# The input projection of an S5 mixer, token-major or feature-major: one stage of a kernel of two transformer blocks

## The chip, the cores and the metric

The kernel runs on one core of a Trainium2 chip. The metric is the device time of one launch in microseconds; less is better. The core has a matrix engine (TensorE, in the profile PE, its weight loads PEld), VectorE (DVE), ScalarE (ACT), GpSimd (POOL) and a queue that issues the transfers (SyncE, SP). Every engine works through its own instructions in order and waits on semaphores for the others.

## What is computed

Two blocks of a float32 model of 1024 tokens and 1024 features: a layer with a gated recurrence and attention, a state-space layer, a feed-forward layer, a mixer layer, and a second feed-forward layer. Only the mixer layer is concerned. Its input projection gives queries, keys, values (512 features each) and u, the input of the S5 mixer. Cut to u:

```python
proj = h @ w_mix_in                       # [1024 tokens, 2048]
q, k, v, u = split(proj, [512, 1024, 1536])
attn = dilated_attention(q, k, v)
# s5_mixer(u): 32 groups of 16 channels, 64 complex states a group
a_bar = exp(dt * a)
b_bar = ((a_bar - 1) / a)[..., None] * b
bu = einsum('bsgc,gpc->bsgp', u, b_bar)
states[t] = a_bar * states[t - 1] + bu[t]  # an associative scan
y = real(einsum('bsgp,gcp->bsgc', states, c)) + d_skip * u
y = gelu(y)
ssm = y * sigmoid(y @ w_glu + b_glu)
mixed = concatenate([attn, ssm]) @ w_mix_out
```

## The kernel before

Activations lie feature-major: eight tiles of 128 features (on partitions) by 1024 tokens, each as a pair (high, low) whose sum is the float32 value, in TensorE's one-pass type. A product is three passes: high times high, high times low, low times high. `proj_fm` makes one tile of 128 output features with the weights as the stationary operand and 512 tokens as the moving one, for all eight feature tiles k.

The mixer layer, `mix_layer`, goes like this. `lead` makes the first two query tiles while the last tokens of the layer before are still being normalised. Then comes the projection to u, then four S5 blocks (`s5_block`) of eight groups, then the other six query and key tiles (`proj_fm`, `stash` spills each as a pair to DRAM), then the values, token-major, then the gating of the S5 output and the attention.

The S5 mixer works on chunks of 8 tokens. The operators of a block of 8 groups (`w1`, `g`, `tp`, `cos`, `sin`, 128 x 1024 each) lie prepared in DRAM and are loaded by SyncE. A block needs its input as `ut`: step and channel on the partitions, group and chunk along the columns. The kernel before gets there in two steps. The projection is token-major: the stationary operand is every eighth token of the activations, so that chunks come out on the partitions, and the weights are the moving operand, 256 columns at a time; then the block transposes U, [chunk, (group, step, channel)], by eight products with the identity.

```python
xh, xl = (get(m, k).rearrange("p (c s) -> p s c", s=8)[:, s, :] for m in "hl")
nc.tensor.matmul(o, xh, wh, start=k == 0, stop=False)
nc.tensor.matmul(o, xh, wl, start=False, stop=False)
nc.tensor.matmul(o, xl, wh, start=False, stop=k == NK - 1)
```

In a block two products, `e` (with `w1`) and `y` (with `tp` and `g`), stand around elementwise work on VectorE: a turn by `cos` and `sin`, a scan along the chunks, a turn back. The block's eight 128 x 1024 tiles are four double tiles of one pool with four buffers, so that a block's loads wait until the block before has released them: the tile of `t1`, `t2` is free when the scan's results are turned back, the other three when the last product `y` is done.

Nobody writes the order of the engines' instructions out: a scheduler sets it from the order of the code, the pools' buffers and its own estimate of times. Weights go through two staging buffers (`wst`), four buffers of high parts and four of low parts; `wload` loads them, scales their rows by a gain on ScalarE (one instruction per feature tile) and splits them. PSUM has two tiles of 1024 columns (`a`) and four of 512 (`b`).

Of the kernel before, what the change touches and what calls it, by code (L numbers as in the profile page):

```python
# [26 lines left out]
# ---------------------------------------------------------------- parameter columns  # L27
# [71 lines left out]
def anchor(K, engine=None):  # L99
    """The last instruction traced on an engine, the tensor engine unless another is given."""  # L100
    for i in reversed(K.nc.cur_bb.bb.instructions):
        if i.engine == (engine or K.pe):
            return i
    return None
# [3 lines left out]
def deferred(K, after):  # L108
    """Loads and fills in the block, which wait for no data, are issued behind `after`
    instead of taking their buffers as soon as one is free."""  # L110
# [13 lines left out]
def marks(K):  # L124
    """The last instructions traced on the engines that do the elementwise work."""
    return [anchor(K, e) for e in (K.act, K.dve, K.pool)]
# [3 lines left out]
def behind(K, ins):  # L130
    """What the block traces is issued behind `ins`, each on its own engine."""
# [6 lines left out]
def split(K, hi, lo, src, eng=None):  # L138
    """hi + lo == src exactly, both in the tensor engine's one-pass type."""
# [4 lines left out]
def scale_rows(K, st, gain, k0, n):  # L144
    """st [128, n, cols] *= the gains of its rows, those of tiles k0 .. k0 + n."""
# [4 lines left out]
def wload(K, src, a, b, gain=None, k0=0):  # L150
    """Weights [128, a, b] with a * b <= 1024 from DRAM, by rows times a gain, as the pair (hi, lo)."""
# [16 lines left out]
def proj_list(K, ps, terms):  # L168
    """ps[f, t] = sum over terms (wh, wl, xh, xl) of w[k, f] x[k, t], three passes each."""
# [12 lines left out]
def lead(K, ws, xt):  # L182
    """Two products of proj_fm at the start of a layer, the first 512 tokens of both ahead of
    the others, which may not be there yet."""
# [11 lines left out]
def transpose_tokens(K, xn, i, XT):  # L196
    """Token tile xn [128 tokens, 1024] -> columns i of the feature-major pair XT."""
# [21 lines left out]
def exp_poly(K, out, x, r, k, ki):  # L219
    """out = exp(x) with x held within +-87, to float32's accuracy; r, k are float and ki  # L220
    integer scratch of x's shape, and out may be x."""
# [14 lines left out]
def softplus(K, out, x, e, s, q, ki):  # L236
    """out = max(x, 0) + log1p(exp(-|x|)); the others are scratch of x's shape (ki integer)."""
# [15 lines left out]
def rsqrt_col(K, out, v, n, scale, eps, mul=1.0, tag="rs"):  # L253
    """out = mul / sqrt(v * scale + eps) on n columns: a first guess from the exponent and
    three Newton steps."""
# [18 lines left out]
def sin_tables(K, pos, cos, sin, ang, n):  # L274
    """cos and sign * sin of the rotary angles, rows as the feature tiles have them."""
# [8 lines left out]
def _parts(*bits):  # L284
    """2 pi as a sum of float32 values, all but the last of so many bits."""
# [11 lines left out]
def reduce_2pi(K, out, ang, n, few=False):  # L297
    """out = ang less a multiple of 2 pi, within +-pi, by steps; n is scratch. `few` says that
    less than 128 turns are taken off."""
# [14 lines left out]
def sin_cos(K, sin, cos, ang, n, sgn, few=False):  # L314
    """sin(sgn * ang) and cos(ang), by steps; n is scratch, and ang may be sin or cos."""
# [7 lines left out]
def conv4(K, out, src, wname, j, nm, bname, copy=False):  # L323
    """Causal conv of 4 taps along tokens for feature tile j of nm (src may be PSUM); with
    `copy` the later taps read a copy of src, which frees it sooner."""
# [11 lines left out]
def attention(K, qb_passes, table, scale, vt, out, p0, ring, chunks):  # L337
    """One head. qb_passes(qb) gives [(stationary [k, 128 queries], moving [k, T keys])];
    table [128, T] is the additive table whose column 896 - 128 qb + key is used;
    vt(kb) is the stationary [128 keys, 64 high | 64 low parts]; out [64, T], whose first  # L340
    partition is p0, takes the transposed result."""
# [51 lines left out]
def layer_a(K, I, XT, get):  # L393
    nc = K.nc
    # feature-major input
# [47 lines left out]
    # low-rank inputs  # L443
# [53 lines left out]
    # gates  # L497
# [14 lines left out]
    # attention operands  # L512
# [81 lines left out]
class Ring:  # L594
    """Runs of columns in turn, from tiles of four rows."""
# [13 lines left out]
class Chunks:  # L609
    """Pairs of transposed probabilities [128, 512] in turn."""  # L610
# [978 lines left out]
def mix_layer(K, I, get, ydram):  # L1589
# [27 lines left out]
    for b in range(4):  # L1617
        s5_block(K, b, U[b])
# [279 lines left out]
```

## Time and profile before

| | us |
|---|---|
| median of 3 runs | 3497.23 |
| fastest and slowest run | 3487.03, 3500.45 |
| span of the profiled execution (first to last instruction) | 3487.5 |
| TensorE busy in the span | 3191.8 (92%) |
| VectorE, ScalarE, GpSimd busy | 2281.8, 1624.8, 741.3 |
| S5 input projection in it | 2267.1 to 2359.6 |
| rest of the stage, to the end of the values | 2359.6 to 2502.1 |

The page gives the span of the profiled execution and no other time of it. Busy time of TensorE includes the overlap of pipelined products, so how fast products follow each other is read from the difference of their starts.

### The profile page before, as it was taken

Reading aid. Unit: us, or ns where it says so; the run is one execution under the profiler, and the core shown is the slowest. Engines: PE = TensorE matmul, PEld = TensorE weight load, DVE = VectorE, ACT = ScalarE, POOL = GpSimd, SP = SyncE. Lnnn points to the kernel's source line nnn. Section 1 sums busy time; section 2 is a strip of 40 time slices with the busy share of each in tenths; the row PEclk is TensorE's granted clock in tenths of the full one; section 3 lists DMA queues with packets and bytes.
Section 4 is the critical chain, followed back from the end, with each engine's and each line's share of the span. In section 5 each row is a group of like instructions: output and inputs, shape, how many; then the busy total and the mean of one; then the engine's idle time right before and its main releaser. Section 6 shows DMA issues by size and latency. Waiting matters only on the chain. (4 is left out here: it accounts for less than half of the span.)

```text
span 3487.5 us, 42834 instructions
## 1 busy us (share of the span) xinstructions
PE 3191.8 (92%) x15848; PEld 2670.7 (77%) x15848; DVE 2281.8 (65%) x3859; ACT 1624.8 (47%) x2971; POOL 741.3 (21%) x455
## 2 busy tenths in 40 slices
PE   8999898999998889879999999799999799999997
PEld 7878776878786867667778777698877578888776
DVE  6537785274747555888775789705676965555998
ACT  5436534253545432455555443523376565554442
POOL 0000010121222111432233434100000332322543
PEclk9999998999999899989999999999999899999999
DMA  3256432132232354223332521314363422223322
GB/s 122 70 205 200 122 122 74 43 70 63 66 71 59 92 168 137 97 76 128 114 117 86 216 79 42 136 46 160 114 186 113 171 79 84 80 91 123 125 79 109
DMA packets 324673, 378.04 MB, mean 108 GB/s; under 512 B 19312, under 2 KB 254960, under 8 KB 324464
## 3 DMA queue, kind: packets, MB, share of 16 engines
q1 hardware_dynamic: 324464, 375.30, 34.5%
q8 instruction: 125, 2.05, 0.2%
q14 instruction: 84, 0.69, 0.1%
HBM read 268.81 MB, written 106.43 MB: 108 GB/s over the span
## 5 line engine op out<-in xcount | busy, mean ns | idle before, releaser
L141 DVE TENSOR_TENSOR wlo<-wst,whi 128x1024 fp32r<-128x1024 f32 (+1 forms) x190 | 228.5, 1206 | 368.1 <-ACT whi L140 367.7
L174 PE MATMUL pa<-x,whi 128*128 128x512 f32 x1440 | 402.0, 399 | 11.0 <-ACT l L332 9.6
L140 ACT ACTIVATE whi<-wst 128x1024 fp32r<-128x1024 f32 (+1 forms) x190 | 180.3, 950 | 419.9 <-PE pa L174 100.3
L174 PEld LDWEIGHTS pa<-x,whi 128*128 128x128 f32 x1440 | 271.4, 191 | 72.1 <-ACT l L332 10.3
L147 ACT ACTIVATE wst<-wst,pk 128x128 f32<-128x128 f32 (+1 forms) x800 | 248.7, 393 | 151.1 <-DMA wst<-in_ffn_w_in_dram 108.4
L174 PE MATMUL pa<-x,wlo 128*128 128x512 f32 x720 | 229.6, 399 | 8.9 <-DVE wlo L141 8.9
L1192 PE MATMUL pa<-x,whi 128*128 128x512 f32 (+1 forms) x736 | 221.7, 384 | 3.5 <-DVE p L1028 2.7
L1192 PE MATMUL pb<-x,whi 128*128 128x512 f32 (+1 forms) x736 | 224.5, 381 | 0.0
L1271 PE MATMUL pa<-wlo,whi 128*128 128x512 f32 x768 | 189.6, 404 | 17.4 <-DVE wlo L141 14.4
L1271 PE MATMUL pb<-wlo,whi 128*128 128x512 f32 x744 | 180.5, 400 | 13.6 <-DVE wlo L141 13.6
L1271 PEld LDWEIGHTS pa<-wlo,whi 128*128 128x128 f32 x768 | 149.5, 196 | 54.9 <-DVE wlo L141 19.7
L1155 POOL TENSOR_TENSOR s<-wst 128x512 f32<-128x512 f32 x44 | 58.3, 1324 | 571.7 <-ACT wst L147 529.4
L1271 PEld LDWEIGHTS pb<-wlo,whi 128*128 128x128 f32 x744 | 142.3, 192 | 47.7 <-DVE wlo L141 17.8
L883 POOL TENSOR_TENSOR s<-s,p 128x1024 f32<-128x1024 f32 x32 | 60.8, 1900 | 542.0 <-DMA s<-d 482.5
L174 PEld LDWEIGHTS pa<-x,wlo 128*128 128x128 f32 x720 | 136.1, 191 | 41.7 <-DVE wlo L141 11.0
L1192 PEld LDWEIGHTS pa<-x,whi 128*128 128x128 f32 x736 | 137.1, 191 | 30.8 <-issue 3.0
L1192 PEld LDWEIGHTS pb<-x,whi 128*128 128x128 f32 x736 | 136.5, 189 | 26.6 <-issue 0.4
L853 PE MATMUL pa<-whi,x 128*128 128x256 f32 x512 | 150.3, 293 | 1.6 <-ACT l L332 1.3
L854 PE MATMUL pa<-wlo,x 128*128 128x256 f32 x512 | 147.1, 287 | 0.0
L855 PE MATMUL pa<-whi,x 128*128 128x256 f32 x512 | 147.1, 287 | 0.0
L140 ACT ACTIVATE whi<-s 128x1024 fp32r<-128x1024 f32 x88 | 93.1, 1058 | 110.1 <-POOL s L1156 52.1
L1192 PE MATMUL pa<-x,wlo 128*128 128x512 f32 (+1 forms) x368 | 141.1, 384 | 2.8 <-DVE wlo L141 2.8
(558 smaller groups left out, 8366.3 us busy)
## 6 DMA issues: line engine op xcount, KB each, us to landing
wst<-in_ffn_w_in_dram SPq DMA_DIRECT2D x88, 512.0 KB, 3.9
d<-p SPq DMA_DIRECT2D x82, 512.0 KB, 3.3
x<-d SPq DMA_DIRECT2D x128, 256.0 KB, 5.4
d<-l SPq DMA_DIRECT2D x63, 512.0 KB, 4.0
p<-d SPq DMA_DIRECT2D x46, 512.0 KB, 4.9
wst<-in_s_w_in_dram SPq DMA_DIRECT2D x40, 512.0 KB, 4.1
s<-d SPq DMA_DIRECT2D x32, 512.0 KB, 9.0
l<-d SPq DMA_DIRECT2D x24, 512.0 KB, 4.3
```

The costliest lines, as they stand in the source:

```text
L140: K.nc.scalar.activation(hi, src, AF.Copy)
L141: (eng or K.nc.vector).tensor_tensor(lo, src, hi.bitcast(F32), ALU.subtract)
L147: K.nc.scalar.activation(st[:, k, :], st[:, k, :], AF.Copy, scale=col(K, gain, k0 + k))
L174: K.nc.tensor.matmul(ps[:, h:h + 512], w, x[:, h:h + 512], start=k == 0 and m == 0, stop=k == n - 1 and m == 2)
L853: nc.tensor.matmul(o, xh, wh, start=k == 0, stop=False)
L854: nc.tensor.matmul(o, xh, wl, start=False, stop=False)
L855: nc.tensor.matmul(o, xl, wh, start=False, stop=k == NK - 1)
L883: nc.gpsimd.tensor_tensor(mv, mv, per_head(csT, P), ALU.subtract)
L1155: G(s1, a21, a22, ALU.add)
L1192: nc.tensor.matmul(p, l[:, k, :], r[:, k, :], start=k + m == 0, stop=k == 3 and m == 2)
L1271: nc.tensor.matmul(bank[j], th[:, a + o:a + o + P], tw[:, b:b + 512], start=c + m == 0, stop=c == n - 1 and m == 2)
```

## The change

The projection to u is made feature-major by `proj_fm`, like the queries and keys: four tiles of 128 features by 1024 tokens, each eight groups of 16 channels. ScalarE copies such a tile from PSUM with the columns reordered from (chunk, step) to (step, chunk), SyncE writes it to DRAM, and the block reads it back by eight loads, one per step, each to 16 partitions (the channels), 8 groups and 128 chunks, which gives `ut` directly. The transposes go. U stays as the place of the block's output. All other lines of the diff only take out comments.

```diff
-def s5_block(K, blk, U):
+def s5_block(K, blk, u_d, U):
...
     w1, gm, tp, ut, cos, sin, t1, t2 = (x[:, j, :] for x in (pa, pb, pc, pt) for j in range(2))
+    by_step = u_d.rearrange("(g c) (s n) -> s c g n", c=16, s=8)
+    for s in range(8):
+        nc.sync.dma_start(ut[16 * s:16 * s + 16].rearrange("p (g n) -> p g n", g=8), by_step[s])
     for n, t in (("w1", w1), ("g", gm), ("tp", tp), ("cos", cos), ("sin", sin)):
         nc.sync.dma_start(t, O[n][blk])
-    for h in range(2):
-        b = K.B()
-        for q in range(4):
-            g = 4 * h + q
-            nc.tensor.transpose(b[:, q * P:(q + 1) * P], U[:, g * P:(g + 1) * P], K.ident)
-        nc.scalar.activation(ut[:, 512 * h:512 * h + 512], b, AF.Copy)
...
-    for hf in range(2):
-        w = [wload(K, w_in[:, 4 * k:4 * k + 4, 1536 + hf * 256:1792 + hf * 256], 4, 256, "mix", 4 * k) for k in range(2)]
-        for h in range(2):
-            a = K.A()
-            for q in range(4):
-                s = 4 * h + q
-                o = a[:, q * 256:q * 256 + 256]
-                for k in range(NK):
-                    wh, wl = (w[k // 4][m][:, k % 4, :] for m in range(2))
-                    xh, xl = (get(m, k).rearrange("p (c s) -> p s c", s=8)[:, s, :] for m in "hl")
-                    nc.tensor.matmul(o, xh, wh, start=k == 0, stop=False)
-                    nc.tensor.matmul(o, xh, wl, start=False, stop=False)
-                    nc.tensor.matmul(o, xl, wh, start=False, stop=k == NK - 1)
-            av = a.rearrange("p (s b g c) -> p s b g c", s=4, b=2, g=8)
-            for b in range(2):
-                ov = U[2 * hf + b].rearrange("p (g s c) -> p s g c", g=8, s=8)[:, 4 * h:4 * h + 4]
-                for q in range(4):
-                    nc.scalar.activation(ov[:, q], av[:, q, b], AF.Copy)
+    u_d = [K.DR([P, T]) for _ in range(4)]
     for b in range(4):
-        s5_block(K, b, U[b])
+        a, u = K.A(), K.L()
+        proj_fm(K, a, wload(K, w_in[:, :, 1536 + b * P:1664 + b * P], NK, P, "mix"), get)
+        nc.scalar.activation(u.rearrange("p (s n) -> p n s", s=8), a.rearrange("p (n s) -> p n s", s=8), AF.Copy)
+        nc.sync.dma_start(u_d[b], u)
+    for b in range(4):
+        s5_block(K, b, u_d[b], U[b])
```

The scheduler orders the stage anew. On TensorE, at the end of the projection before: the last strided products, the transposes of block 0 (L1553), the first query tile (L174), and in it block 0's first products `e` (L1561) and the first part of `y` (L1583).

```order
L1611 MATMUL pa_17229<-whi_17115,x_16212 128x256
L1553 MATMUL pb_17343<-ident,r_16872 128x128 x4
L1553 MATMUL pb_17349<-ident,r_16872 128x128 x4
L174 MATMUL pa_17606<-x_16209,whi_17608 128x512 x2
...
L174 MATMUL pa_17606<-x_16209,wlo_17609 128x512 x2
L1561 MATMUL pb_17355<-p_17335,p_17334 128x128 x4
L1561 MATMUL pb_17363<-p_17335,p_17334 128x128 x4
L1583 MATMUL pb_17382<-p_17335 128x128
```

And now: the last products of the fourth projection to u (L174, weights 17079 and 17080), at once block 0's `e` (now L1559) and the first part of `y` (now L1581), then the first query tile.

```order
L174 MATMUL pa_17076<-x_16210,whi_17079 128x512 x2
L174 MATMUL pa_17076<-x_16212,whi_17079 128x512 x2
L174 MATMUL pa_17076<-x_16210,wlo_17080 128x512 x2
L1559 MATMUL pb_17159<-p_17143,p_17142 128x128 x4
L1559 MATMUL pb_17167<-p_17143,p_17142 128x128 x4
L1581 MATMUL pb_17186<-p_17143 128x128
L1581 MATMUL pb_17196<-p_17143 128x128
L174 MATMUL pa_17398<-x_16209,whi_17400 128x512 x2
```

The transposes are gone, and block 0's first products stand behind all four projections, where 24 products of the first query tile stood between.

On SyncE, the loads of block 1 before: two operators (L1548) between the spills of the query tiles (L634, L635), and three more further on.

```order
L634 DMA d_16722<-l_17669 128x1024
L156 DMA wst_18024<-in_w_mix_in_dram 128x4x256
L635 DMA d_16723<-l_17670 128x1024
L1548 DMA p_17402<-d_11593 128x1024
L1548 DMA p_17402<-d_11594 128x1024
L634 DMA d_16724<-l_17738 128x1024
L156 DMA wst_18034<-in_w_mix_in_dram 128x4x256
L635 DMA d_16725<-l_17739 128x1024
L1548 DMA p_17403<-d_11595 128x1024
L1548 DMA p_17404<-d_11596 128x1024
L1548 DMA p_17404<-d_11597 128x1024
```

And now: eight loads of u (L1550, from 16875, the second tile of u) and one operator (now L1552, 11595 is `tp`) into one double tile, a spill, then `w1`, `g`, `cos`, `sin` into the two others.

```order
L634 DMA d_16722<-l_17461 128x1024
L156 DMA wst_17816<-in_w_mix_in_dram 128x4x256
L1550 DMA p_17207<-d_16875 16x8x128 x8
L1552 DMA p_17207<-d_11595 128x1024
L635 DMA d_16723<-l_17462 128x1024
L1552 DMA p_17206<-d_11593 128x1024
L1552 DMA p_17206<-d_11594 128x1024
L1552 DMA p_17208<-d_11596 128x1024
L1552 DMA p_17208<-d_11597 128x1024
```

The first free tile takes u and `tp` where it took `w1` and `g`, and four operators, not three, stand behind it. Downstream, from the gating to the end, the order is the same but for some neighbours that change places around the gating and in the first tiles of the second feed-forward layer.

## Rows read from the trace of the kernel before

**Rows 1.** The page's first line.
```profile
span 3487.5 us, 42834 instructions
```
**Rows 2.** Stages: us; PE, PEld, DVE, ACT, POOL busy; clock; DMA share; GB/s.
```profile
2267.10:2359.60 92.50, 92.48 (x384) 92.50 (x385) 6.05 (x5) 18.65 (x61) 0.00 (x0) 1.00 0.14 43
2359.60:2420.00 60.40, 60.40 (x318) 51.59 (x318) 40.60 (x41) 26.66 (x54) 0.00 (x0) 1.00 0.43 149
2420.00:2440.00 20.00, 19.49 (x111) 16.72 (x110) 8.72 (x10) 5.84 (x10) 0.00 (x0) 1.00 0.61 228
2440.00:2460.00 20.00, 18.95 (x150) 18.22 (x149) 11.01 (x11) 5.21 (x7) 0.00 (x0) 1.00 0.56 198
2460.00:2480.00 20.00, 17.43 (x146) 17.22 (x146) 18.06 (x24) 4.18 (x9) 0.00 (x0) 1.00 0.10 35
```
**Rows 3.** One line's instructions: weight loads of L1609, ns min/median/max, first and last start.
```profile
L1609 PEld LDWEIGHTS pa<-whi,x x128: 313/337/341, 2267.1 to 2358.8; 128*128 128x128 f32 x128
```
**Rows 4.** Timeline of TensorE, projection's first and last product: start us, us, instruction.
```profile
2267.12 0.49 PE L1609 MATMUL pa<-whi,x 128*128 128x256 f32 x1 [0.46 <-DVE l L141]
...
2359.37 0.41 PE L1611 MATMUL pa<-whi,x 128*128 128x256 f32 x1
```
**Rows 5.** Timeline of TensorE: transposes, the line behind them, six query products.
```profile
2359.62 1.03 PE L1553 MATMUL pb<-ident,r 128*128 128x128 f32 x8
2360.41 1.17 PE L174 MATMUL pa<-x,whi 128*128 128x512 f32 x4
...
2412.21 1.07 PE L174 MATMUL pa<-x,whi 128*128 128x512 f32 x4
...
2413.57 1.07 PE L174 MATMUL pa<-x,whi 128*128 128x512 f32 x4
```
**Rows 6.** Timeline of TensorE, the values: first and last of 18 products.
```profile
2499.96 0.28 PE L1636 MATMUL pa<-whi,x 128*128 128x256 f32 x1
...
2502.00 0.28 PE L1638 MATMUL pa<-whi,x 128*128 128x256 f32 x1
```
**Rows 7.** Timeline of VectorE, starts and ends of the blocks' work; idle before in brackets.
```profile
2367.07 0.69 DVE L1563 TENSOR_TENSOR p<-pb,p 128x512 f32<-128x512 f32 x1 [3.10 <-PE pb L1561]
...
2385.75 0.07 DVE L1578 MEMSET p<- 128x8 f32 x1
...
2398.57 0.69 DVE L1563 TENSOR_TENSOR p<-pb,p 128x512 f32<-128x512 f32 x1 [9.89 <-PE pb L1561]
...
2416.74 0.07 DVE L1578 MEMSET p<- 128x8 f32 x1
...
2430.68 0.69 DVE L1563 TENSOR_TENSOR p<-pb,p 128x512 f32<-128x512 f32 x1 [11.49 <-DMA p<-d]
```
**Rows 8.** Timeline of SyncE's queue: small writes of the preparation; loads of blocks 1, 2.
```profile
1628.20 5.03 SPq L1527 DMA_DIRECT2D d<-l  x8
...
2385.75 0.81 SPq L1548 DMA_DIRECT2D p<-d  x2
...
2391.75 1.32 SPq L1548 DMA_DIRECT2D p<-d  x3
...
2422.10 1.34 SPq L1548 DMA_DIRECT2D p<-d  x3
```
**Rows 9.** One line, L1527: its transfers from issue to landing.
```profile
DMA to landing us min/median/max: 1.8/2.3/3.6
```
**Rows 10.** Transfers of 2355 to 2500: spills, count, size, median us to landing.
```profile
d<-l SPq DMA_DIRECT2D x12, 512.0 KB, 3.8
```
**Rows 11.** Chain of waits ahead of the stage: start us, us, what.
```profile
2242.27 6.33 DMA wst<-in_w_mix_in_dram
```
**Rows 12.** Timeline of ScalarE: scalings of weights; two strided splits of 512 columns.
```profile
2248.69 1.70 ACT L147 ACTIVATE wst<-wst,pk 128x256 f32<-128x256 f32 x4 [5.09 <-DMA wst<-in_w_mix_in_dram]
...
2271.24 2.45 ACT L147 ACTIVATE wst<-wst,pk 128x128 f32<-128x128 f32 x8 [2.74 <-DMA wst<-in_w_mix_in_dram]
...
2501.47 2.07 ACT L140 ACTIVATE x<-pb 128x512 fp32r<-128x512 f32 x2
```

## The prediction

> **What bounds the kernel now.** I read the table of the span by stages first, since the change touches one stage only. From 2267.1 us, where the S5 input projection begins, to 2502.1, where the last product of the values ends, TensorE is busy 92.48 of 92.5 us in the projection and all 60.4 of the next 60.4; only between 2420 and 2480 does it stand still, 0.51, 1.05 and 2.57 us, 4.1 in all, and the granted clock is 1.00 in every stage, the higher of its two levels, 2.4 GHz [rows 2]. So in this stage a TensorE microsecond taken away is one of the span, as long as nothing else is right behind it. The span is 3487.5 us [rows 1]. The page gives no other time for that execution; the runs shown are 3487.03 to 3500.45, median 3497.23, so the median lies 9.7 us above the span. I take the difference as the same after the change and subtract from the median what I subtract from the span.
>
> What is right behind TensorE is the chain of the four S5 blocks. VectorE starts a block at 2367.07, 2398.57 and 2430.68, a pitch of 31.5 and 32.1 us. A block's elementwise work takes 18.7 us (2367.07 to the memset at 2385.75); the rest of the pitch is a hole of 12.8 and 13.9 us in front of the next block (2385.75 to 2398.57, 2416.74 to 2430.68) in which the next block's operators are loaded [rows 7]. SyncE shows why: two loads go out at once when the scratch tile is free (2385.75), the other three only at 2391.75, when the last products have released the other tiles [rows 8]. The chain ends at present well ahead of the values. After the change it starts earlier too, but both shrink towards each other, and that is the question.
>
> **The projection itself.** It is 384 products of 256 columns, first at 2267.12, last at 2359.37, the next line's start at 2359.62 [rows 4]: 92.5 us, 0.241 us each. The token-major values, also 256 columns wide but with contiguous stationary tiles, go at (2502.00 - 2499.96) / 17 = 0.12 us [rows 6]: the strided stationary operand, every eighth token, costs half of the time, its load takes 337 ns [rows 3], longer than the product's pitch, and seems to set it. The new form is four times `proj_fm`, 4 x 8 x 3 x 2 = 192 products of 512 columns. The same helper runs in the queries and keys of this stage, six products in 2413.57 - 2412.21 = 1.36 us, 0.227 each [rows 5]. 192 x 0.227 = 43.5. **Gain 49.0 us.**
>
> **The transposes of the input.** 32 go (four blocks, eight each). Eight take 2360.41 - 2359.62 = 0.79 us [rows 5], so **3.2 us**; all stand in TensorE's order between other products. On ScalarE their eight evacuations and the 32 copies of the old projection go, and four copies with a stride come. A strided copy is bounded by the strided split, two of 512 columns in 2.07 us, so about 2.1 for 1024 [rows 12], and from below by half of that. ScalarE is busy 18.65 of the 92.5 us and 26.66 of the 60.4 [rows 2], and the PSUM tile that the copy frees is wanted one projection (10.9 us) later: nothing.
>
> **The way through DRAM.** A tile u is written (a 512 KB write lands after 3.8 us [rows 10]) and read back by eight loads of 16 partitions, with a wait on SyncE for the write in between. The nearest row is the eight writes of like shape in the preparation, 5.03 us of issue for eight [rows 8], landing 1.8 to 3.6 us after issue [rows 9]; they overlapped, since eight in a row would not fit into that. For block 0: projection 0 ends at 2267.1 + 10.9 = 2278.0, the copy at about 2281 (it is behind a split on ScalarE), the write lands at 2285, the eight loads at 2293, the four operators behind them by 2300. In TensorE's order the block's first products stand behind all four projections, at 2310.6: covered by 10 us. If that cover were gone, TensorE would wait in front of them. Behind SyncE's wait stand the writes of u 1 to 3 and the weights of the fourth and later query tiles, wanted from 2346 on; two weight tiles are ahead of it.
>
> For blocks 1 to 3 it is no longer covered for nothing. SyncE's order now has eight loads of u and one operator into the first free tile, and four operators, not three, behind the release of the others. The eight take 5.0 us of issue [rows 8]; the release comes 6.0 us after the tile is free (2385.75 to 2391.75 [rows 8]), so the four go out hardly later than the three did, but the second sine half lands one 512 KB load later. Three loads needed 2398.57 - 2391.75 = 6.8 us to the first use: 2.3 each as they come, 2 to 3 more for the fourth. The added price per block lies between 0 and 5 (the issue not covered at all); I take 2.5, from the rows of the same queue: the hole becomes 15.8, the pitch 34.5.
>
> **TensorE against the chain.** The order of the changed kernel puts between the starts of the blocks 90 + 30, then 90 + 42 products of 0.227, then 36 of them and 134 of 0.12: 27.2, 29.9, 24.2 us. The blocks' own small products are what is left of the old stage: 142.5 (2359.62 to 2502.1) less 288 x 0.227 = 65.3, less 384 x 0.12 = 46.1, less 3.2 and 4.1 idle gives 23.8, 6.0 a block. So TensorE's pitches are 33.2, 35.9, 30.2 against 34.5 of the chain. It waits about 1.5 in block 0 (the copy of the decays stands on ScalarE behind weights that come late through SyncE), 1.3 in block 1, nothing in block 2, 4.3 in block 3, 7 in all against 4.1 now: **a loss of 3 us**. Behind the last wait stand 96 products of the values, 11.5 us, where 145 stand now: the chain is nearer to the end.
>
> **Ahead of the stage.** ScalarE scales the new weights in eight steps, 2.45 us, not four, 1.70 [rows 12], 0.75 more a tile, and this stands before the last two normalised token tiles, for which the second half of `lead` waits. But that wait ended with a weight load, issued at 2242.27 and landed 6.33 us later [rows 11], which stood on SyncE behind a load of an S5 operator; now it stands behind the last write of x3, ready about 1.5 us earlier, and two operator loads no longer run beside it. Between 2.4 earlier and 2 later; I take **1.2 us earlier**. In the first tiles of the second feed-forward layer a dozen instructions change places; nothing in the rows prices that, and I keep it at nothing, 4 us either way.
>
> **Sum.** -49.0 - 3.2 + 3.0 - 1.2 = -50.4: span 3437.1, median 3497.2 - 50.4 = **3447 us**. Own range: all idle gone and the lead 2.4 earlier, -58.7, to idle of 17, -40: 3438 to 3457, and the 4 us of the second layer either way.
>
> **Rivals.**
> The chain takes over. If the four operators come one behind the other at the pace of the later row, 8.6 us for three (2422.10 to 2430.68 [rows 7, 8]), 2.9 each, and the issue of the eight is not covered, the hole is 19 and the pitch 38. From block 0's end at 2334.5 the last block's products come at 2334.5 + 3 x 38 = 2448.5, with 3.5 for them and 11.5 of values the stage ends at 2463.5, 38.6 before now: 3459. For it speaks that VectorE already waited 11.5 us for a load [rows 7]; against it that DMA stands at 0.43 to 0.61 of its time [rows 2].
>
> The eight small loads run one after another. This is the slower end: at the median of 2.3 us [rows 9] 18.4 for a tile, then five operators at 2.9, a hole of 33, a pitch of 52; the end is 2334.5 + 156 + 15 = 2505, no change, 3500. At the longest landing, 3.6 each, the pitch is 62 and the end 2535: 3530. It decides from a pitch of 51. Against it: the like eight were issued in 5.03 us and each landed within 3.6 [rows 8, 9].
> The Trainium skill speaks for this rival and against the change: SBUF — State Buffer, under "Can I just issue two DMAs to hit both halves?", says that two loads to different partitions all but serialize, and its "Summary: rules for kernel authors" asks for 128 partitions and one DMA, not several. By that rule the 3500 of this case would come out. The landings in the trace do not bear it out for pieces this small.
>
> The weights come late. Each new tile needs a 512 KB load, 2.45 of scaling and two splits within 10.9 us, where a pair was wanted every 46 before. SyncE's waits for u could hold a load back; a full 10 us for each of two tiles costs 20: 3467. Against it: the query tiles have kept that pace, TensorE without idle from 2359.6 to 2420 [rows 2].
>
> That the change does not do what it says cannot be seen here: the strided operand is gone from the order.
>
> **How the numbers follow.** Forecast 0.74, chain 0.16, weights 0.05, serial loads 0.05, of which 0.03 slower. A measurement of this kernel can't tell less than 0.5%, 17 us, from no change. The first three are faster by more: faster 0.94 (some weight cases end near the bound), same 0.03, slower 0.03. The range goes from the forecast's lower end, with the second layer's 4 us and the run-to-run difference of the median, 3430, to the chain's 3459 with the same above, 3466.
>
> **What would show it.** Right: no LDWEIGHTS of 337 ns in the projection, TensorE at 0.227 us a product for 43.5 us, blocks of the chain 34 to 35 us apart, TensorE idle of 5 to 9 us to the last value, that end near 2452. Wrong: idle in front of the blocks' products that the loads of u release, a pitch of 38 and over, holes between the four projections, a fall of the granted clock below 1.00, or a loss behind 2452 that takes back part of the 50.

## The result and the profile after

| | before | after |
|---|---|---|
| median of 4 runs, us | 3492.67 | 3437.26 |
| fastest and slowest run, us | 3487.03, 3500.45 | 3432.02, 3444.89 |
| span of the profiled execution, us | 3487.5 | 3430.2 |
| stage, start of the projection to the last value, us | 234.9 | 184.6 |
| TensorE idle in the stage, us | 4.1 | 6.1 |

The ratio of the medians is 0.9845, with a 95% interval from 0.9824 to 0.9866. In a second set of runs of both kernels it was 0.984, from 0.9825 to 0.9855. The change saves about 55 us; 3447 was forecast, within 3430 to 3466.

The page's first line of the kernel after, for [rows 1]:

```profile
span 3430.2 us, 42421 instructions
```

The span is cut into four pieces by three marks that both traces have: the first product of `lead` (line L191), the first product of the projection, and the end of the stage, taken as 0.12 us behind the start of the last product of the values. To the first mark there are 2222.53 us before and 2220.53 after. The order of the compute engines up to there is the same, SyncE has one operator load of block 0 there where it had three, and the twelve profiled executions of this document took from 2220 to 2241 us to this mark, the changed kernel's own two 2220.5 and 2227.7: the 2.0 us are no more than executions differ. From the first mark to the projection's start there are 44.59 and 39.64. From there to the stage's end, 235.00 and 184.71. What follows takes 985.4 and 985.3. So of the 57.3 us between the two profiles 50.3 lie in the stage and 5.0 in the lead.

The stage of the kernel after by windows (us; PE, PEld, DVE, ACT, POOL busy; granted clock; DMA share; GB/s), for [rows 2]:

```profile
2260.10:2303.70 43.60, 43.59 (x193) 36.08 (x193) 6.03 (x5) 20.37 (x40) 0.00 (x0) 1.00 0.63 198
2303.70:2340.00 36.30, 33.44 (x172) 28.01 (x171) 20.95 (x21) 16.53 (x30) 0.00 (x0) 1.00 0.41 133
2340.00:2360.00 20.00, 19.01 (x94) 15.82 (x93) 15.48 (x16) 6.48 (x12) 0.00 (x0) 1.00 0.49 180
2360.00:2380.00 20.00, 19.79 (x112) 16.97 (x112) 6.38 (x7) 6.47 (x10) 0.00 (x0) 1.00 0.77 275
2380.00:2400.00 20.00, 19.24 (x132) 17.78 (x131) 17.37 (x19) 2.92 (x3) 0.00 (x0) 1.00 0.35 122
2400.00:2420.00 20.00, 18.70 (x159) 18.53 (x159) 8.89 (x14) 4.60 (x10) 0.00 (x0) 1.00 0.45 158
2420.00:2445.00 25.00, 25.00 (x214) 25.00 (x213) 12.95 (x20) 5.47 (x12) 0.00 (x0) 1.00 0.07 22
```

The first row is the projection: 192 products in 43.6 us with nothing idle, and 0.63 of the DMA time in use where it was 0.14. The lost time of the rest of the stage is the difference between the first two figures of the other rows, 2.86, 0.99, 0.21, 0.76 and 1.30, 6.1 in all: 3.2 of it in front of the first products of blocks 1 to 3, 1.9 in front of the second products (`y`) of blocks 0 and 2, 1.0 for a PSUM tile that VectorE still had to split. The clock is 1.00 throughout, its higher level, as before.

Start and end of the projection on TensorE, for [rows 4]; L1559 is the first product of block 0:

```profile
2260.17 1.17 PE L174 MATMUL pa<-x,whi 128*128 128x512 f32 x4
...
2303.81 1.95 PE L1559 MATMUL pb<-p,p 128*128 128x128 f32 x16
```

Starts (L1561) and ends (L1576) of the blocks' work on VectorE, for [rows 7]:

```profile
2308.50 0.69 DVE L1561 TENSOR_TENSOR p<-pb,p 128x512 f32<-128x512 f32 x1
...
2327.69 0.07 DVE L1576 MEMSET p<- 128x8 f32 x1
...
2342.06 0.69 DVE L1561 TENSOR_TENSOR p<-pb,p 128x512 f32<-128x512 f32 x1 [5.82 <-DMA p<-d]
...
2361.79 0.07 DVE L1576 MEMSET p<- 128x8 f32 x1
...
2377.75 1.22 DVE L141 TENSOR_TENSOR wlo<-wst,whi 128x1024 fp32r<-128x1024 f32 x1 [13.51 <-ACT whi L140]
...
2380.03 0.68 DVE L1561 TENSOR_TENSOR p<-pb,p 128x512 f32<-128x512 f32 x1
...
2398.83 0.07 DVE L1576 MEMSET p<- 128x8 f32 x1
...
2411.46 1.29 DVE L1561 TENSOR_TENSOR p<-pb,p 128x512 f32<-128x512 f32 x2 [4.90 <-DMA p<-d]
```

The holes in front of blocks 1 to 3 are 14.4, 18.2 and 12.6 us, the pitches 33.6, 38.0 and 31.4. The 18.2 has a cause of its own, and the row of L141 shows it: VectorE had a split of weights in front of block 2, and waited 13.51 us for ScalarE, which waited for a load of weights. SyncE's queue shows where that load stood:

```profile
2361.75 4.82 SPq L1550 DMA_DIRECT2D p<-d  x8
2366.61 0.43 SPq L1552 DMA_DIRECT2D p<-d  x1
...
2368.04 1.28 SPq L156 DMA_DIRECT2D wst<-in_w_mix_in_dram  x1
2369.41 3.07 SPq L1552 DMA_DIRECT2D p<-d  x4
```

It is behind the eight loads of u (L1550), whose issue takes 4.82 us, and ScalarE could use its weights only at 2375. So here, by the order on SyncE, the way through DRAM reaches the chain of the blocks. TensorE lost only 0.2 us in front of this block, since query products stood ahead of it; in front of blocks 1 and 3, where VectorE's rows name the operators' loads, 1.67 and 1.30.

### The profile page after: what moved, and what is told of

Same layout as the page of the kernel before. It is cut to its first block, busy times and chain, and to the rows that moved or that the text cites. A ratio compares the mean times of both kernels' runs of the same rounds, so it can differ in the third digit from the quotient of the medians.

```text
span 3430.2 us, 42421 instructions
## 1 busy us (share of the span) xinstructions
PE 3134.3 (91%) x15624; PEld 2608.4 (76%) x15624; DVE 2283.8 (67%) x3859; ACT 1623.5 (47%) x2951; POOL 740.0 (22%) x455
## 5 line engine op out<-in xcount | busy, mean ns | idle before, releaser
L141 DVE TENSOR_TENSOR wlo<-wst,whi 128x1024 fp32r<-128x1024 f32 (+1 forms) x190 | 227.7, 1202 | 337.7 <-ACT whi L140 337.6
L174 PE MATMUL pa<-x,whi 128*128 128x512 f32 x1568 | 433.0, 397 | 11.6 <-ACT l L332 9.5
L174 PEld LDWEIGHTS pa<-x,whi 128*128 128x128 f32 x1568 | 294.8, 190 | 77.8 <-ACT l L332 10.4
L140 ACT ACTIVATE whi<-wst 128x1024 fp32r<-128x1024 f32 (+1 forms) x190 | 179.9, 948 | 355.9 <-PE pa L174 94.1
L174 PE MATMUL pa<-x,wlo 128*128 128x512 f32 x784 | 249.2, 398 | 9.6 <-DVE wlo L141 9.6
L1192 PE MATMUL pb<-x,whi 128*128 128x512 f32 (+1 forms) x736 | 224.1, 381 | 0.0
L1192 PE MATMUL pa<-x,whi 128*128 128x512 f32 (+1 forms) x736 | 221.4, 383 | 2.2 <-DVE p L1028 1.9
L1271 PEld LDWEIGHTS pa<-wlo,whi 128*128 128x128 f32 x768 | 150.5, 197 | 54.0 <-DVE wlo L141 19.2
L174 PEld LDWEIGHTS pa<-x,wlo 128*128 128x128 f32 x784 | 147.9, 190 | 44.6 <-DVE wlo L141 11.5
L1192 PEld LDWEIGHTS pa<-x,whi 128*128 128x128 f32 x736 | 136.8, 190 | 29.4 <-issue 3.0
L1192 PEld LDWEIGHTS pb<-x,whi 128*128 128x128 f32 x736 | 136.0, 188 | 26.4 <-issue 0.4
L140 ACT ACTIVATE whi<-s 128x1024 fp32r<-128x1024 f32 x88 | 93.0, 1057 | 111.9 <-POOL s L1156 59.5
L1192 PE MATMUL pa<-x,wlo 128*128 128x512 f32 (+1 forms) x368 | 141.2, 384 | 4.4 <-DVE wlo L141 4.4
```

What stands on the lines that cost most here:

```text
L140: K.nc.scalar.activation(hi, src, AF.Copy)
L141: (eng or K.nc.vector).tensor_tensor(lo, src, hi.bitcast(F32), ALU.subtract)
L174: K.nc.tensor.matmul(ps[:, h:h + 512], w, x[:, h:h + 512], start=k == 0 and m == 0, stop=k == n - 1 and m == 2)
L1192: nc.tensor.matmul(p, l[:, k, :], r[:, k, :], start=k + m == 0, stop=k == 3 and m == 2)
L1271: nc.tensor.matmul(bank[j], th[:, a + o:a + o + P], tw[:, b:b + 512], start=c + m == 0, stop=c == n - 1 and m == 2)
```

## The experiments

Each run's lead (first product of L191 to the projection's start), stage (to the start of the last product of the values), TensorE's idle time in it and the holes in front of blocks 1 to 3 are read from its own trace, in us. What lies ahead of the lead differs by execution, from 2220 to 2241 us as told above, and hides a few microseconds in the whole time. The kernels e2, e3, e4, e5, e10 and e11 were run once each, so their whole times decide nothing.

| kernel | lead | stage | idle | holes |
|---|---|---|---|---|
| before | 44.6 | 234.9 | 4.1 | 12.8, 13.9, 9.8 |
| after | 39.6 | 184.6 | 6.1 | 14.4, 18.2, 12.6 |
| after_again | 40.5 | 185.6 | 6.9 | 15.7, 18.1, 13.3 |
| e1_contiguous | 42.6 | 189.6 | 3.7 | 12.8, 13.8, 9.8 |
| e10_stride2 | 42.3 | 190.0 | 3.9 | 12.8, 14.1, 9.9 |
| e11_stride4 | 42.7 | 231.7 | 3.9 | 12.8, 13.9, 9.9 |
| e2_operators_later | 38.6 | 234.6 | 3.7 | 12.8, 13.9, 9.9 |
| e3_no_dram | 40.0 | 176.3 | 0.0 | 14.0, 14.3, 11.9 |
| e4_twice | 39.9 | 181.6 | 4.2 | 18.8, 18.7, 15.9 |
| e8_pool_queue | 39.5 | 180.6 | 2.8 | 13.8, 16.6, 15.5 |
| e5_write_ordered | 39.5 | 181.4 | 3.2 | 15.8, 13.2, 11.3 |
| e6_pairs | 40.4 | 186.4 | 7.5 | 12.7, 11.9, 10.6 |

**Is it the stride, or the width?** In the kernel before, the stationary operand becomes 128 neighbouring tokens:

```
-  xh, xl = (get(m, k).rearrange("p (c s) -> p s c", s=8)[:, s, :] for m in "hl")
+  xh, xl = (get(m, k)[:, s * P:(s + 1) * P] for m in "hl")
```

> The kernel before, still token-major with 384 products of 256 columns, but the stationary operand of the projection to u is 128 neighbouring tokens, not every eighth; the tokens of u are therefore in the wrong places. Theory (the stride of the stationary operand sets the pace): the weight loads of the projection fall from 337 ns to about 190, its products come every 0.12 us as the values' do, the projection takes 384 x 0.12 = 46 us and not 92.5, and nearly the whole 46 us arrives in the span: 3492.7 - 46 = about 3447, ratio 0.987. Rival (the width is to blame: 256 columns a product are too few to hide a weight load, whatever its stride): the pitch stays at 0.24 us, the projection at 92 us, the time within 0.3% of before. Second rival (the chain of the four blocks takes the gain back): the projection takes 46 us but the idle of TensorE in the stage rises from 4 us by 15 or more, and the time falls by 30 at most.

Median of 4 runs 3454.38 us against 3501.22 before, ratio 0.9859, from 0.9836 to 0.9881. One row of its trace (ns min/median/max of the weight loads, first and last start), for [rows 3]:

```profile
L1609 PEld LDWEIGHTS pa<-whi,x x128: 186/192/193, 2273.8 to 2319.4; 128*128 128x128 f32 x128
```

Weight loads of 192 ns, a projection from 2273.78 to 2319.93, 46.15 us or 0.120 a product. The stride was what cost; the width of 256 columns is innocent, and the chain took nothing back (idle 3.7). About 47 of the change's 55 us come with this edit alone. The rest of the stage's gain over it, 5.0 us (189.6 to 184.6), is 2.5 for the wider product (46.15 to 43.64), about 3 for the transposes and 1.7 of a lowered clock that this execution had once, for 3.4 us at half of the rate near 2437, less 2.4 more idle.

**How much stride?** The same edit with runs of 256 and 512 tokens, of which every second or fourth is taken:

```
+  xh, xl = (get(m, k)[:, s // 2 * 256:s // 2 * 256 + 256].rearrange("p (c t) -> p t c", t=2)[:, s % 2, :] for m in "hl")
...
+  xh, xl = (get(m, k)[:, s // 4 * 512:s // 4 * 512 + 512].rearrange("p (c t) -> p t c", t=4)[:, s % 4, :] for m in "hl")
```

> The kernel before, with every second token of a run of 256 as the stationary operand of the projection to u in place of every eighth; the tokens of u stand in wrong places. Measured so far: 337 ns a weight load at a step of eight, 192 at a step of one. Theory (any step other than one costs the same): 337 ns, pitch 0.241, projection 92 us. Rival (the cost grows with the step): between 192 and 337 ns, about 200 to 260, pitch 0.12 to 0.19 us, projection 46 to 73 us.

> The same with every fourth token of a run of 512. Theory (any step other than one costs the same): 337 ns, 92 us. Rival (the cost grows with the step): above what the step of two takes and below 337 ns, about 240 to 300, projection 60 to 85 us.

The same row of the step of two, then of the step of four:

```profile
L1609 PEld LDWEIGHTS pa<-whi,x x128: 195/195/197, 2275.9 to 2321.6; 128*128 128x128 f32 x128
```

```profile
L1609 PEld LDWEIGHTS pa<-whi,x x128: 311/329/332, 2274.8 to 2363.7; 128*128 128x128 f32 x128
```

Neither the theory nor its rival fits both runs: the theory fails at a step of two, the rival, which stood at 60 to 85 us, at four. A step of two (8 bytes) costs next to nothing, 195 ns and 46.2 us of projection; a step of four (16 bytes) already costs nearly what eight does, 329 against 337 ns, and 89.7 us. So the cost is neither that of any step nor one that grows evenly with it: there is an edge between 8 and 16 bytes. The Trainium skill has such an edge for another engine's own programs (GPSIMD Engine Reference, "7. Performance pitfalls for Q7 kernels": reads whose step is over 8 bytes cost half as much again); the rows above show one at the same place for TensorE's weight loads, at 1.7 times the cost.

**What shortened the lead?** The kernel before, with only block 0's five operator loads put behind the lead:

```
...
+  with deferred(K, K.led if blk == 0 else None):
       for n, t in (("w1", w1), ("g", gm), ("tp", tp), ("cos", cos), ("sin", sin)):
           nc.sync.dma_start(t, O[n][blk])
...
```

> The kernel before, with only the five operator loads of block 0 moved on SyncE behind the lead. Between the lead's first weight row on TensorE and the start of the projection to u lie 44.6 us in the kernel before and 39.6 in the changed one. Theory (the operator load ahead of the fourth weight load, and the two that run beside it, delay the lead): that stretch falls by 4 to 5 us, to about 40, the fourth weight load is issued about 17 us after the lead's first instruction and not 19.7, and lands in about 4 us and not 6.3. Rival (the shape of the weight tiles or the changed order of writes in the lead does it): the stretch stays at 44 to 45. The time itself, 0 to 5 us below before, cannot tell them apart; the stretch is read from the profile.

The lead fell to 38.6 us. The chain's wait of before was for the fourth weight load [rows 11]; here are the four loads and the operators on SyncE after the edit:

```profile
2229.18 0.38 SPq L156 DMA_DIRECT2D wst<-in_w_mix_in_dram  x1
...
2232.47 0.38 SPq L156 DMA_DIRECT2D wst<-in_w_mix_in_dram  x1
...
2239.67 0.38 SPq L156 DMA_DIRECT2D wst<-in_w_mix_in_dram  x1
...
2243.11 0.38 SPq L156 DMA_DIRECT2D wst<-in_w_mix_in_dram  x1
...
2245.99 3.61 SPq L1549 DMA_DIRECT2D p<-d  x5
```

The fourth goes out 13.9 us after the first product of L191 (2229.24), where it was 19.7 in the kernel before and 17.1 in the one after (about 17 was expected), lands after 4.9 us where it was 6.3 and 4.0 (about 4 was expected), and ScalarE's last scaling no longer waits for it. The rival, 44 to 45, is out. Against the profile of before the edit gives 6.0 us; e1, e10 and e11, whose lead has the order of before, took 42.6, 42.3 and 42.7, so 4 us is the better size. The seven executions with the changed order lie between 39.5 and 40.5, 3.1 us below the mean of the four with the old one. The gain here is real, a by-product of where the scheduler puts the operators once the block no longer asks for them early.

**What does the way through DRAM cost?** u is kept on the chip, and ScalarE copies it to the operand tile:

```
-  nc.sync.dma_start(u_d[b], u)
...
-  for s in range(8):
-      nc.sync.dma_start(ut[16 * s:16 * s + 16].rearrange("p (g n) -> p g n", g=8), by_step[s])
+  nc.scalar.activation(ut, U, AF.Copy)
```

> The changed kernel, with u kept in the block's own tile on the chip and copied by ScalarE into the operand tile in place of the write to DRAM and the eight loads; the move of the rows to (step, channel) is left out. Theory (the way through DRAM costs about 2 us of hole a block, 14.4, 18.2 and 12.6 us now against 12.8 and 13.9 before): holes fall to 11 to 14, TensorE's idle in the stage from 6 to 3 to 5 us, the stage from 184.7 to 181 to 184. Rival (the way costs nothing, and the 18.2 us hole is the pools' release): holes and stage stay within 1 us. Second rival (the way holds much back): the holes fall below 9 and the stage by more than 4 us.

Its stage as one window (columns as above):

```profile
2280.08:2456.42 176.34, 176.34 (x1055) 157.54 (x1056) 88.01 (x99) 67.18 (x118) 0.00 (x0) 1.00 0.40 139
```

All idle time of the stage is gone, more than the theory gave (3 to 5 left), and the middle hole falls by 4 us. The stage falls by 8.3 us, which the second rival had, but not by its holes below 9. So the way costs about 6 us of TensorE time: 176.3 against 184.6 is this 6.1, 0.5 of five transposes of the gating that the scheduler moved behind the stage, and 1.6 by which the other products follow each other a little faster. Little of it arrives: from the projection's start to the last product of the attention (L388) there are 409.2 us, against 407.5 and 410.2 in the two profiles of the changed kernel, and to the end of the span 1167.5 against 1170.1 and 1172.5. Of 8 to 9 us won in the stage 4 to 6 are lost behind it; that is taken up below.

The eight loads issued twice:

```
+  for s in range(8):
+      nc.sync.dma_start(t2[16 * s:16 * s + 16].rearrange("p (g n) -> p g n", g=8), by_step[s])
```

> The changed kernel, with the eight loads of u issued a second time in each block, into a scratch tile that is overwritten later. Theory (the loads are covered in block 0 and pass their issue time on to the holes of blocks 1 to 3): each of those three holes grows by the 4 to 5 us that eight issues take, the pitches of 33.6, 38.0 and 31.4 become 37 to 42, and TensorE's idle in the stage grows from 6 us to 9 to 18; block 0's first products do not wait for u. Rival (there is slack, the loads run beside the wait for the pools): holes and idle stay within 1.5 us. Second rival (small loads run one behind another at 2.3 us each): the holes grow by 18 us, the stage by 30 or more.

Two holes grow by 3.3 and 4.4 us, about as the theory says, the middle one by 0.5: there the second eight are issued behind the weight load, for which VectorE waits here too (11.52 us). Nothing grows by 18, so the loads do not run one behind another. The idle part of the theory fell: 4.2 us, not 9 to 18, and the stage is 3 us shorter, not longer. The scheduler knows the loads and moves query and value products ahead of the blocks (48, 48 and 76 stand in front of blocks 1 to 3 where the changed kernel has 30, 42 and 44), so that a later block need not mean an idle TensorE. What more a hole costs can't be read from this run.

**Is it the issue on SyncE?** The same eight loads, issued by GpSimd:

```
-  nc.sync.dma_start(ut[16 * s:16 * s + 16].rearrange("p (g n) -> p g n", g=8), by_step[s])
+  nc.gpsimd.dma_start(ut[16 * s:16 * s + 16].rearrange("p (g n) -> p g n", g=8), by_step[s])
```

> The changed kernel, with the eight loads of u in each block issued by GpSimd, which has no work in this stage, and not by SyncE. Theory (it is the 4 to 5 us that eight issues take on SyncE which delay the weight load and the operators behind them): the hole of 18.2 us before block 2 falls to about 14, the others by 0 to 2, the idle of TensorE in the stage from 6 to 1 to 3 us; in time 3 to 5 us less than the changed kernel, about 0.1%. Rival (the holes come from the transfers themselves, not from their issue): holes and idle stay within 1 us. Second rival (loads issued by GpSimd start later or slower): holes grow by 2 us or more, idle over 8.

The repeated kernel first:

> The changed kernel once more, beside the three below, to see what one execution differs from the next. Lead (first instruction to the start of the projection) within 1 us of 39.6, projection 43.6 us, idle of TensorE to the last value 5 to 7 us, holes within 1 us of 14.4, 18.2 and 12.6. If the holes scatter by more than 2 us, the order of late transfers is chance, and differences of that size between kernels mean nothing.

Its median is 3445.85 us against 3500.77 before; lead, stage, idle and holes agree with the first profile within 1.4 us, where the holes were expected within 1. With GpSimd issuing, idle falls to 2.8 us, the middle hole only to 16.6, the last one grows by 2.9 to 15.5, and the time is the same, 3446.64 us (ratio to before 0.984 for both, from 0.9823 to 0.9856 here). The lower idle can't be put down to the issue alone, since the scheduler has here 39, 46 and 87 products in front of blocks 1 to 3. Its queue around block 2, GpSimd and then SyncE and ScalarE:

```profile
2377.88 4.17 POOL L1550 DMA_DIRECT2D p<-d  x8 [27.83 <-DVE p L1576]
```

```profile
2378.67 0.38 SPq L156 DMA_DIRECT2D wst<-in_w_mix_in_dram  x1
```

```profile
2388.43 1.71 ACT L147 ACTIVATE wst<-wst,pk 128x256 f32<-128x256 f32 x4 [6.93 <-DMA wst<-in_w_mix_in_dram]
```

The weights now go out 1.3 us after the scratch tile is free (2377.32), not 6.3; but their scaling starts 9.8 us after the issue, where it was 7.0 (2368.04 to 2375.07). One line of each trace, L1550, shows the loads of u beside them, SyncE's first, then GpSimd's:

```profile
DMA to landing us min/median/max: 2.2/2.5/3.7
```

```profile
DMA to landing us min/median/max: 3.4/7.1/8.8
```

So both the theory and its second rival have a part: the issue did hold the weights back, and of the 4.9 us that it frees, 2.7 are given back while the loads of u, the operators and the weights are under way together. That the slow landing is a matter of GpSimd's queue isn't shown: in front of block 2 SyncE's last four operator loads, too, took 8.9 to 10.4 us here, 6.6 to 8.0 in the changed kernel, and in front of block 3, with fewer loads of weights and operators beside them, GpSimd's took 3.4 to 5.0.

**Reordering at the write.** Eight writes of u in the block's order and one load; and with it another pairing of the pool's tiles:

```
-  nc.sync.dma_start(u_d[b], u)
+  by_group = u_d[b].rearrange("(s c) (g n) -> g c s n", c=16, g=8)
+  for g in range(8):
+      nc.sync.dma_start(by_group[g], u[16 * g:16 * g + 16].rearrange("p (s n) -> p s n", s=8))
...
-  w1, gm, tp, ut, cos, sin, t1, t2 = (x[:, j, :] for x in (pa, pb, pc, pt) for j in range(2))
+  w1, ut, tp, gm, cos, sin, t1, t2 = (x[:, j, :] for x in (pa, pb, pc, pt) for j in range(2))
...
-  for n, t in (("w1", w1), ("g", gm), ("tp", tp), ("cos", cos), ("sin", sin)):
+  for n, t in (("w1", w1), ("cos", cos), ("sin", sin), ("tp", tp), ("g", gm)):
```

> The first of the two edits alone: eight writes of u in the block's order, one load in the block. Theory: the 18.2 us hole falls by the 4 us of issue to about 14, the idle of TensorE to 2 to 4 us. Rival (it is the release of the pool's tiles alone): holes as before, 14, 18 and 13, idle 6.

> The changed kernel with two edits. The reordering of u moves to the write: eight writes of 16 partitions put it into DRAM in the order that the block wants, so that the block reads it with one load of 128 partitions. And the tile of u shares its double tile with the first operator, and the load order follows the order of use. Theory (the issue of eight loads and the late release of the pool's tiles make the holes): holes of 9 to 13 us, no idle of TensorE over 1 us in front of a block, 1 to 3 us idle in all, stage 3 to 5 us shorter than 184.6. Rival (what the writes cost more, eight issues each in the projection, comes back as late weights there): gaps between the four parts of the projection, 44 to 50 us and not 43.6, no gain. In time neither can be more than 0.2%.

With the writes alone the middle hole falls to 13.2 us and the idle to 3.2, as the theory had it. But block 0 now has all of that idle: its work on VectorE takes 26.2 us (2323.69 to 2349.89), not 19.2, for late weights stand in the midst of it; their scalings start 13.4 and 14.6 us apart (2300.65, 2314.04, 2328.62), where one part of the projection takes 10.9. With the pairing the holes are shorter than in the changed kernel, 12.7, 11.9 and 10.6, and the idle is 7.5, 3.4 of it in block 0 and 1.2 to 1.5 in front of each later one: the theory's holes, not its time. In both, 1.7 us of the stage are a lowered clock, which fell for 3.4 us about when this long wait in block 0 ended. The rival is wrong too in its place, since no gap opened between the parts of the projection; its cause, late weights, is right. The median of the version with the pairing is 3462.22 us, ratio 0.9882, from 0.9862 to 0.9902: worse than the changed kernel, 3445.85 in the same set, in every one of the four runs of each. Of the 20.8 us between the profiles of these two, 13.1 lie ahead of the lead, where the order is the same and executions differ, 0.7 in lead and stage, and 7.1 behind the stage; so it is the stretch behind the stage that shows something of the edit. Here is the rest of the mixer, from the last value to the last product of the attention, before, after and with the ordered writes alone (columns as in the windows above):

```profile
2502.00:2722.72 220.72, 203.20 (x1216) 171.63 (x1215) 152.17 (x315) 141.35 (x288) 0.00 (x0) 1.00 0.55 159
```

```profile
2444.76:2667.63 222.87, 206.07 (x1219) 175.66 (x1218) 152.31 (x315) 141.25 (x288) 0.00 (x0) 0.98 0.55 158
```

```profile
2460.39:2694.30 233.91, 212.93 (x1224) 180.12 (x1223) 152.63 (x315) 145.16 (x290) 0.00 (x0) 0.95 0.52 150
```

It is 11.0 us longer with the ordered writes than in the changed kernel, at the same work but for five transposes: 4.2 more of it idle (233.91 - 212.93 against 222.87 - 206.07) and 6.9 more of it busy, at a clock of 0.95 and not 0.98, which would make about 7 (0.05 x 233.9 less 0.02 x 222.9). From the first score product (L359) to the last L388 it is 204.1 us in e5 and 205.0 in e6, 203.1 in e3, 201.4 in e4, but 194.7 and 196.3 in the changed kernel, 196.9 in e8, 192.5 before. In the first four the scheduler set another order behind the stage too, one and the same for all four. From the last value to the end of the span these four took 991.2 to 995.0 us; the changed kernel took 985.5 and 986.9, e8, with nearly its order, 988.5. In e4 the clock of the window above is 0.98, as in the changed kernel, and the window is still 8.3 us longer, 6.6 of it idle: so the order costs time without the clock. Why the clock is lower in the other three is open. No version here is shown to beat the changed kernel in time.

## Why the prediction was right

The gain forecast, 50.4 us, was about 5 us short of the measured 55, and the time, 3447, about 10 above the measured 3437, since with a fourth run the median of the kernel before came out 4.6 lower. Range, sign and main mechanism held. By its steps:

- **The projection, 49.0 us.** Measured 92.5 to 43.64, 48.9. That the stride sets the old pace was inferred from the values' pitch and the length of the weight loads; e1 shows it. The new pace, 0.227 us a product, was that of the same helper in the same stage, and it came out to the digit.
- **The transposes, 3.2 us.** Busy time of TensorE in the stage falls from 230.75 to 178.47, 52.3; 48.9 of it are the projection's and 3.4 the rest: 2.9 for the starts of the 32 transposes, and 0.5 for three transposes of the gating that now stand behind the stage.
- **The way through DRAM.** Block 0: loads of u at 2277.15, the operators issued by 2283.4, products wanted at 2303.81. The last operator landed 7.6 us after its issue, at 2290.5, so the cover was 13 us where 10 was forecast. The copy took 2.03 us where 2.1 was the bound. The rows of the copy and of the queue:

```profile
2271.94 2.03 ACT L1602 ACTIVATE l<-pa 128x1024 f32<-128x1024 f32 x1
...
2274.00 0.32 SPq L1603 DMA_DIRECT2D d<-l  x1
2274.41 0.39 SPq L156 DMA_DIRECT2D wst<-in_w_mix_in_dram  x1
2277.15 4.32 SPq L1550 DMA_DIRECT2D p<-d  x8
2281.56 1.80 SPq L1552 DMA_DIRECT2D p<-d  x4
```

- **The chain, a pitch of 34.5.** Measured 33.6, 38.0 and 31.4, a mean of 34.3. The mean was right and its working was not: the prediction gave each block the same 2.5 us more, while the holes grew by 1.6, 4.3 and 2.9, and the cause of the 4.3 was not the operators' loads but a weight load that stood behind the eight issues. That the mean agrees so well is luck. The prediction's upper bound, 5, was the issue of the loads "not covered", and that is near to what happened in front of block 2.
- **Idle, 7 against 4.1.** Measured 6.1 and 6.9. Block 0's wait of 1.5 for the decays is there (1.19), for the reason given, and block 1's of 1.3 (1.67). But of the 4.3 in front of block 3 only 1.30 came, and 1.0 for the PSUM tile and 1.0 in block 2 were not forecast: here too the sum is right and not all of its parts.
- **The lead, 1.2 us.** This is the mis-sized term. It measured 5.0 between the first two profiles and 3.1 between the means of all executions with the old order and with the new. The mechanism was the named one: e2, which moves the operator loads and nothing else, gives it all. Which part is the load that stood ahead of the weights and which the loads beside them, e2 does not tell. "Between 2.4 earlier and 2 later" was too narrow: the weight load went out 2.7 us earlier, where 1.5 was expected, and landed 2.3 us faster besides (6.33 us to land before, 3.99 after).
- **The second feed-forward layer, nothing within 4.** From the stage's end there are 985.4 and 985.3 us, but only since two differences cancel: 3.7 us more from there to the first product of that layer (L1192), 3.7 less behind it. Neither was forecast, and the zero is luck. In the attention the granted clock was 0.98 where it had been 1.00, and e1 and e8 show the same 0.98; the prediction named a fall of the clock as a way to lose part of the gain. The stretch from the last value to the last L388 is 2.2 us longer in the first profile of the changed kernel, 3.8 in the second and 4.7 in e1, whose order there is that of before; so 2 to 4 us of the gain may be lost there. That the shorter stage is the reason isn't shown: in e10, with nearly the stage of e1, the stretch is as short as before.
- **Rivals.** The chain taking over: its pitch of 38 came, once, not three times; the sum stayed with the forecast. Serial loads: eight were issued in 3.6 to 4.9 us and each landed within 3.7, all eight within 6.9 of the first issue. The rule of the Trainium skill (SBUF — State Buffer, "Can I just issue two DMAs to hit both halves?"), which spoke for it, does not hold for eight loads of 16 partitions here; e4, with sixteen, says the same. Weights late: yes, by a few microseconds in blocks 0 and 2, never between the projection's four parts.

## What to carry to other kernels

Look at the duration of the weight loads beside that of the products: where a load takes longer than the pitch that its width should give, it sets the pace, and the operand's step is the first suspect; here a step of 8 bytes was free, 16 bytes was not. Data that need another layout can go through DRAM if other products stand between write and use: here the last load of u landed 11.5 us after the copy out of PSUM began, and in block 0 three parts of the projection, 10.9 us each, covered that. What is paid then is queue time, since many small issues delay the loads behind them; all in all the way cost some 6 us of the stage. And where a scheduler orders the program, compare stages between marks, not whole times: edits that won 3 to 8 us in their stage (e3, e4, e5) lost 4 to 10 behind it, in an order that they changed there.

## What was not expected of the hardware

A stationary operand read with a step of two 4-byte elements loads in 195 ns, as a contiguous one does (192); with four it takes 329, with eight 337. A copy on ScalarE that writes with a step of 512 bytes, 128 by 1024, took 2.03 us (L1602), twice the 1.0 of a contiguous one, also out of PSUM (L140). Eight loads of 64 KB issued by GpSimd took 0.53 us each to issue and 7.1 to land (medians of 32), against 0.43 and 2.5 from SyncE; more of the operators' and weights' loads ran beside them, so the two causes are not told apart.
